# Late weight combinations in small steps, later stores, and output weights kept one chunk later, in a gated hybrid decoder step on one core

## The chip, the cores and the metric

The kernel runs on one core of a Trainium2 chip. The metric is the device time of one execution in microseconds (us). The engines are TensorE (PE, matmuls), VectorE (DVE), ScalarE (ACT), GpSimd (POOL) and SyncE (SP). All DMA transfers of this kernel are issued from SP's queue, which works in order: an issue that waits for its semaphore holds up everything behind it.

## The reference

One layer of a decoder step on 4096 prompt tokens (model width 1024) and 8 sample tokens, all in float32:

```python
h = rmsnorm(x) @ w_in        # columns: u | z_pool | q | k | v | z_attn | g_pool | g_attn
pooled  = multiscale_pool(u)                    # trailing means over 2/4/8/16, minus u itself
att     = sliding_window_attention(q, k, v)     # window 128, 8 query heads, 2 kv heads, sinks, T5 bias
br_pool = (grouped(pooled) * pool_scale * silu(z_pool)) @ w_br_pool
br_attn = (att * silu(z_attn)) @ w_br_attn
merged  = sigmoid(g_pool) * br_pool + sigmoid(g_attn) * br_attn
y       = rmsnorm(x + merged @ w_out)
```

The last keys, values and pool inputs are also outputs.

## The kernel before

**Precision.** A float32 product is made of three matmuls (lines 177 to 179, `mm3`): weights and activations are split into a rounded high part and a low part, and high x high, high x low and low x high are added up. `split_into` (lines 137 to 139) makes a weight's two parts: ACT casts the high part (line 138), DVE or POOL subtracts for the low part (line 139). A split weight tile `w` holds [128, 2, 4, 128], 512 KB; the raw tile `wr` that it comes from holds 256 KB.

**Chunks.** The prompt is worked through in eight chunks of 512 tokens; the second one also carries the eight sample tokens (520 columns, in two halves of 260). In each chunk the input projection is done in pairs of 128-column tiles. A pair is a 2 x 2 block product; `Pair` does it either with seven block products on combined weights (`s1` to `s4`, sums and differences of the raw blocks) and three plain blocks (`11`, `12`, `22`), or, for the pairs listed in `EIGHT` and in the first chunk only, with eight block products on plain weights. Each block product is 12 matmuls.

**Combined weights.** In the first chunk a seven-product pair loads its four raw blocks (line 193; tags `wr` and `wr0`, four buffers each, in turns), adds and subtracts them on DVE (line 198, scratch tag `sr`, one buffer), splits the results into `w` tiles, uses them, and `kept` stores them to DRAM (line 171, `ss<-w`). Later chunks load the stored 512 KB (line 167, `w<-ss`). For the four pairs in `EIGHT` the combined weights aren't used in the first chunk; `combine` makes them late in that chunk, one pair at a time, in split tiles with the tag `sc`, which has one buffer, and stores them (`ss<-sc`).

**Order within a chunk.** First K and V, Q, and the first A pair. Then eight fill stages (`FILL`): a projection pair on PE, into which attention scores, transposes and the value products of 128-token blocks are woven. In the first chunk these fill pairs make their combined weights on DVE and ACT, which also do the attention's element-wise work. Then come the gate pairs and the branch products `branch(0)` to `branch(7)` (line 854, `mm<-yph`, `mm<-yah`), and eight output tiles e = 0 to 7 (line 896, `mm<-mh`, with two weight tiles each). At each even e the next chunk's activations are prepared (`prep_xt`, lines 396 to 439).

**Output weights.** `kept` is used for them too: the first chunk splits each raw half and stores it (`so<-w`, 16 stores), and later chunks load 512 KB each (`w<-so`).

**Buffers.** Split weights share five `w` buffers; from the second chunk three more (`w2`) are used, in space that the first chunk's own pool (`wr0`, `sr`, `sc`) gives up when it is closed by `more_weights`.

A scheduler lays out each engine's instructions, in the order of the program where nothing else is ready sooner. Each engine then works through its list in order. A tile's buffer comes free when all that read it, stores included, are done.

The late calls stand in the branch loop and in the output loop of the first chunk:

```python
for j in range(KT):
    branch(j)
    if later and j > 4:
        combine(later.pop(0))
...
for e in range(KT):
...
    if later and e in (1, 3, 5):
        combine(later.pop(0))
```

Of the kernel before, what the change touches and what calls it, by code (L numbers as in the profile page):

```python
# [10 lines left out]
F32 = mybir.dt.float32  # L11
F32R = mybir.dt.float32r
AF = mybir.ActivationFunctionType
ALU = mybir.AluOpType
# [4 lines left out]
P = 128  # L19
# [16 lines left out]
W_U, W_Z, W_Q, W_K, W_V, W_A, W_GP, W_BR, W_GA, W_O = 0, 4, 8, 12, 13, 14, 18, 26, 34, 42  # L36
# [5 lines left out]
T_1, T_2, T_3, T_4, B_11, B_21, B_22 = range(7)  # L42
HB = TP // 2

EIGHT = [W_K, W_Q, W_U, W_U + 2]
SW = 16 + TP


def split_kernel(ctx, tc, i, o):
    nc = tc.nc  # L50
# [5 lines left out]
    dp = ctx.enter_context(tc.tile_pool(name="dp", bufs=1, space=DRAM))  # L56
# [6 lines left out]
    def st(shape, tag, bufs, dt=F32, nm=None):  # L63
        cnt[0] += 1
        return sp.tile(shape, dt, tag=tag, name=f"{nm or tag}_{cnt[0]}", bufs=bufs)
# [53 lines left out]
    def fst(shape, tag, bufs, dt=F32):  # L119
        cnt[0] += 1  # L120
        return p0.tile(shape, dt, tag=tag, name=f"{tag}_{cnt[0]}", bufs=bufs)
# [15 lines left out]
    def split_into(w, raw, eng=None):  # L137
        nc.scalar.copy(w[:, 0], raw)  # L138
        (eng or nc.vector).tensor_tensor(out=w[:, 1], in0=raw, in1=w[:, 0].bitcast(F32), op=ALU.subtract)  # L139

    def wtile():
        if "p1" in place:
            place["n"] += 1
            if place["n"] % 8 >= 5:
                cnt[0] += 1
                return place["p1"].tile([P, 2, 4, P], F32R, tag="w2", name=f"w_{cnt[0]}", bufs=3)
        return st([P, 2, 4, P], "w", 5, F32R)

    def wraw(idx, half):
        raw = st([P, 4, P], "wr", 4)  # L150
        nc.sync.dma_start(out=raw, in_=i["wall"][idx][:, 4 * half:4 * half + 4, :])
        return raw

    def wquarter(idx, half, eng=None):

        raw = wraw(idx, half)
        w = wtile()
        split_into(w, raw, eng)
        return w

    cache = {}

    def kept(key, make, own=False):

        w = fst([P, 2, 4, P], "sc", 1, F32R) if own else wtile()
        if key in cache:
            nc.sync.dma_start(out=w.bitcast(F32), in_=cache[key])
            return w
        split_into(w, make())
        cache[key] = dp.tile([P, 2, 4, P], F32, tag=f"s{key}", name=f"s{key}")  # L170
        nc.sync.dma_start(out=cache[key], in_=w.bitcast(F32))
        return w

    def mm3(ps, w, nk, rhs, start=True, stop=True, k0=0, **kw):
# [9 lines left out]
    def segs(c):  # L184
        return [(0, HB), (HB, TP)] if c == CS else [(0, T)]

    def combined(ia, ib, own=False):

        odd = own or len(cache) // 4 % 2
        raw = {}  # L190
        for idx, half in ((ib, 0), (ib, 1), (ia, 0), (ia, 1)):
            raw[idx, half] = fst([P, 4, P], "wr0", 4) if odd else st([P, 4, P], "wr", 4)
            nc.sync.dma_start(out=raw[idx, half], in_=i["wall"][idx][:, 4 * half:4 * half + 4, :])
        a11, a12, a21, a22 = raw[ia, 0], raw[ia, 1], raw[ib, 0], raw[ib, 1]
        s = fst([P, 4, P], "sr", 1)

        def add(o_, x, y, op):
            nc.vector.tensor_tensor(out=o_, in0=x, in1=y, op=op)
            return o_
        make = {"s1": lambda: add(s, a21, a22, ALU.add), "s2": lambda: add(s, s, a11, ALU.subtract),  # L200
                "s3": lambda: add(a21, a11, a21, ALU.subtract), "s4": lambda: add(s, a12, s, ALU.subtract)}
        plain = {"11": a11, "12": a12, "22": a22}
        return make, plain

    class Pair:
# [3 lines left out]
        def __init__(self, c, ia, ib, off=0, eng=None):  # L209
            self.c, self.ia, self.ib, self.eng = c, ia, ib, eng  # L210
            self.eight = c == 0 and ia in EIGHT
            self.pre = {}
# [104 lines left out]
    def first_tile(what, g):  # L317
        if what in ("gp", "ga"):
            return (W_GP if what == "gp" else W_GA) + 2 * g
        return {"a": W_A, "u": W_U, "z": W_Z}[what] + g  # L320

    def combine(ia):

        make, _ = combined(ia, ia + 1, True)
        for q in ("s1", "s2", "s3", "s4"):
            kept(f"{q}_{ia}", make[q], True)

    def pair(c, ia, **kw):
        p_ = Pair(c, ia, ia + 1, **kw)
# [44 lines left out]
    def prep_sq(c, parts, place_=None):  # L374

        if 0 in parts:
            state["ss"] = st([P, 10], "ss", 2)
        ss = state["ss"]
        for m in parts:
            t, half = m // 2, m % 2  # L380
            p = P if t < NB else NS
            xr = place_[m] if place_ else st([P, 4, P], "wr", 4).rearrange("p k c -> p (k c)")
            src = i["xq"][c, t] if t < NB else i["xn"]
            nc.sync.dma_start(out=xr[0:p], in_=src[:, half * T:(half + 1) * T])
            nc.scalar.activation(out=xr[0:p], in_=xr[0:p], func=AF.Square, accum_out=ss[0:p, m:m + 1])
# [244 lines left out]
    for c in range(NCH):  # L630
# [41 lines left out]
        w = TP if smp else T  # L672
# [12 lines left out]
        for j in (0, 2):  # L685
# [3 lines left out]
            if j == 0:  # L689
# [3 lines left out]
                for g in range(2):  # L693
# [4 lines left out]
                                                   in1=vs[:, 1:, g, r].bitcast(F32),  # L698
# [89 lines left out]
        def gate(which, p, **kw):  # L788
            idx = first_tile(which, p)
            return Pair(c, idx, idx + 1, **kw)  # L790

        later = list(EIGHT) if c == 0 else []

        def gate_done(which, p, h):
            nc.scalar.activation(out=h, in_=h, func=AF.Tanh, scale=0.5)
# [8 lines left out]
        for hb in range(2 * NB):  # L804
            what, g = FILL[hb]
            idx = first_tile(what, g)
            x = Pair(c, idx, idx + 1, off=16 if what == "u" else 0, eng=att)
# [25 lines left out]
        x = gate("ga", 1)  # L833
# [33 lines left out]
        gate_pair("gp", 2)  # L867
        for j in range(KT):
            branch(j)
            if later and j > 4:  # L870
                combine(later.pop(0))
            if nxt and j < 4:
                prep_sq(nxt, [2 * j, 2 * j + 1] + ([8, 9] if nxt == CS and j == 3 else []))
            if j == 1:
                gate_pair("ga", 2)
            if j == 3:
                gate_pair("gp", 3)
                gate_pair("ga", 3)
            if nxt and j == 4:
                prep_rs(nxt)  # L880
            if nxt and j == 5:
                state["rsb"] = rstd_bc(nxt, state["rs"])
# [3 lines left out]
        for e in range(KT):  # L886
            if e % 4 == 0:
                oy[e // 4] = big([P, 4, TP], F32, f"oy{e // 4}")
            if e % 2 == 0:
                xt = pair_tile()[:, :, 0:T]  # L890
                nc.sync.dma_start(out=xt, in_=i["xt"][c, :, e:e + 2, :])
            wo = [kept(f"o{e}_{half}", lambda: wraw(W_O + e, half)) for half in range(2)]
            for a, b in segs(c):
                ps = ps_mm(b - a)
                for half in range(2):
                    mm3(ps, wo[half], 4, lambda k: (mh[half][:, k, a:b], ml[half][:, k, a:b]),
                        start=half == 0, stop=half == 1)
                f = min(b, T)
                y = oy[e // 4]
                nc.vector.tensor_tensor(out=y[:, e % 4, a:f], in0=ps[:, 0:f - a], in1=xt[:, e % 2, a:f], op=ALU.add)  # L900
                if b > T:
                    nc.vector.tensor_tensor(out=y[:, e % 4, T:TP], in0=ps[:, f - a:], in1=xs0[:, e, :], op=ALU.add)
            n = w
            tail = c == NCH - 1 and e == KT - 1
            if e % 2 == 0 and c == NCH - 1 and e == KT - 2:
                sq = pair_tile()[:, :, 0:n]
                nc.scalar.activation(out=sq[:, 0], in_=y[:, e % 4, 0:n], func=AF.Square)
            if tail:
                nc.scalar.activation(out=sq[:, 1], in_=y[:, e % 4, 0:n], func=AF.Square)
            if e % 2 == 1:  # L910
                if not tail:
                    sq = pair_tile()[:, :, 0:n]
                    nc.scalar.activation(out=sq, in_=y[:, e % 4 - 1:e % 4 + 1, 0:n], func=AF.Square)
                if e == 1:
                    nc.vector.tensor_tensor(out=acc[:, 0:n], in0=sq[:, 0], in1=sq[:, 1], op=ALU.add)
                else:
                    for s_ in range(1 if tail else 2):
                        nc.vector.tensor_tensor(out=acc[:, 0:n], in0=acc[:, 0:n], in1=sq[:, s_], op=ALU.add)
                if c == NCH - 1 and e in (1, 5):
                    v = {1: 1, 5: 4}[e]  # L920
                    nc.scalar.activation(out=y[:, v % 4, 0:n], in_=y[:, v % 4, 0:n], func=AF.Identity,
                                         scale=gf[:, v:v + 1])
            if nxt and e % 2 == 0:
                prep_xt(nxt, e // 2)
            if later and e in (1, 3, 5):
                combine(later.pop(0))
        if c == 0:
            more_weights()
        final = (c, acc, oy, n)
# [72 lines left out]
```

## Time and profile before

| | us |
|---|---|
| median of 3 runs | 2447.07 |
| lowest, highest | 2443.22, 2449.73 |
| profiled execution | 2449.79 |
| its span | 2448.0 |

| engine | busy us (share of the span) |
|---|---|
| PE, matmuls | 2343.5 (96%) |
| PE, weight loads | 2180.9 (89%) |
| DVE | 1645.0 (67%) |
| ACT | 1152.9 (47%) |
| POOL | 312.2 (13%) |

The queue of dynamic transfers moved 587.09 MB, at a share of 70.2% of the 16 DMA engines. The mean granted TensorE clock was 0.987 of full speed. The first chunk ends at about 377 us of the span, where the first matmuls of the second chunk stand.

A line of an engine's timeline is read as: start us, duration us, engine, line of the kernel, operation, output <- inputs, shapes, count, and in brackets the idle time just before it with the instruction that ended it. A line of waits is: who waited <- for whom: total us, times, longest us. In a table of windows each row is a stretch of time with each engine's busy us and, in brackets, its instructions, and then the granted clock, the DMA share and GB/s.

### The profile page before, as it was taken

The numbers are of one execution on the slowest core, as the hardware profiler recorded it, in microseconds if no ns is written. First come the engines' busy times: TensorE is split into PE (matmuls) and PEld (weight loads), VectorE is DVE, ScalarE is ACT, GpSimd is POOL, SyncE is SP. The second block draws the span as 40 slices with busy tenths as digits, with TensorE's granted clock in tenths as the row PEclk, the third lists the DMA queues.
The fourth block names the chain that finished last, engine by engine and source line by source line (L and its number), as shares of the span: only waits on it lengthen the run. The fifth ranks groups of instructions, "written<-read, shape, count | busy, mean of one in ns | idle before, by whom it ended". The sixth has DMA issues, their size and how long they took to land.

```text
span 2448.0 us, 44073 instructions
## 1 busy us (share of the span) xinstructions
PE 2343.5 (96%) x16559; PEld 2180.9 (89%) x16559; DVE 1645.0 (67%) x3207; ACT 1152.9 (47%) x2346; POOL 312.2 (13%) x258
## 2 busy tenths in 40 slices
PE   7989968999999999999999999999999999999998
PEld 6988858999999988999889998899988998899996
DVE  7888866765567756686566765678557775568652
ACT  6666524564246632465334652356424564245531
POOL 1000000310014100230003300032000410013000
PEclk9999989999999999999999999999999999999998
DMA  6647898866687766866678666776677766677654
GB/s 225 216 172 250 282 311 310 233 241 234 213 272 257 245 221 228 299 234 225 224 245 288 234 236 224 241 278 231 239 236 244 273 224 236 238 281 242 219 191 146
DMA packets 235360, 589.90 MB, mean 241 GB/s; under 512 B 36699, under 2 KB 39036, under 8 KB 235148
## 3 DMA queue, kind: packets, MB, share of 16 engines
q1 hardware_dynamic: 235148, 587.09, 70.2%
q8 instruction: 131, 2.15, 0.4%
q14 instruction: 81, 0.66, 0.1%
HBM read 522.59 MB, written 64.40 MB: 240 GB/s over the span
## 4 chain that ended last, share of the span: by engine, by line
PE 69%; DVE 14%; DMA 9%; ACT 4%; issue 3%; SPq 0%; POOL 0%; DVEq 0%; ACTq 0%; POOLq 0%
PE hb L177 12%; PE hb L178 12%; PE hb L179 12%; PE mm L177 8%; PE mm L179 8%; PE mm L178 8%; DMA H<-in_xt 3%; DMA wr<-in_xq 3%; DVE w L139 2%; PE tp L485 2%; PE pv L496 2%; DMA wr<-in_wall 1%; DVE H L727 1%; DVE oy L618 1%; ACT w L138 1%
## 5 line engine op out<-in xcount | busy, mean ns | idle before, releaser
L177 PE MATMUL hb<-xt,w 128*128 128x256 f32 x3316 | 940.2, 284 | 33.4 <-DVE H L299 20.6
L179 PE MATMUL hb<-xt,w 128*128 128x256 f32 x3316 | 933.3, 282 | 4.8 <-DVE w L139 4.8
L178 PE MATMUL hb<-xt,w 128*128 128x256 f32 x3316 | 935.6, 282 | 0.3
L177 PEld LDWEIGHTS hb<-xt,w 128*128 128x128 f32 x3316 | 627.7, 189 | 44.5 <-DVE H L299 24.8
L179 PEld LDWEIGHTS hb<-xt,w 128*128 128x128 f32 x3316 | 629.3, 190 | 7.1 <-DVE w L139 6.5
L178 PEld LDWEIGHTS hb<-xt,w 128*128 128x128 f32 x3316 | 628.1, 189 | 3.7 <-DVE xt L182 1.5
L138 ACT CAST w<-wr 128x512 fp32r<-128x512 f32 x570 | 350.6, 618 | 340.6 <-PE hb L179 209.8
L139 DVE TENSOR_TENSOR w<-wr,w 128x512 fp32r<-128x512 f32 x402 | 275.3, 689 | 143.1 <-ACT w L138 138.8
L139 POOL TENSOR_TENSOR w<-wr,w 128x512 fp32r<-128x512 f32 x168 | 253.0, 1508 | 481.0 <-ACT w L138 384.7
L177 PE MATMUL mm<-mh,w 128*128 128x512 f32 (+1 forms) x576 | 216.5, 376 | 25.5 <-ACT w L138 24.6
L179 PE MATMUL mm<-mh,w 128*128 128x512 f32 (+1 forms) x576 | 215.5, 374 | 0.1
L178 PE MATMUL mm<-ml,w 128*128 128x512 f32 (+1 forms) x576 | 214.3, 372 | 0.0
L337 POOL TENSOR_TENSOR rs<-rs,nhalf 128x4 f32<-128x4 f32 (+1 forms) x18 | 18.0, 1002 | 1344.2 <-DVE rs L335 1344.2
L855 DVE SCALAR_TENSOR_TENSOR H<-H,mm 128x512 f32<-128x512 f32 (+1 forms) x144 | 90.3, 628 | 111.7 <-PE mm L179 111.2
L466 ACT ACTIVATE LL<-LL,nm 128x257 f32<-128x257 f32 (+1 forms) x256 | 126.5, 496 | 65.5 <-DVE nm L463 65.4
L177 PEld LDWEIGHTS mm<-mh,w 128*128 128x128 f32 x576 | 109.9, 191 | 46.3 <-ACT w L138 26.0
L423 ACT CAST xt<-H 128x256 fp32r<-128x256 f32 (+6 forms) x92 | 63.2, 687 | 169.3 <-DVE H L412 122.2
L177 PE MATMUL mm<-xt,w 128*128 128x260 f32 x476 | 135.5, 285 | 5.1 <-DMA w<-ss 3.0
L178 PE MATMUL mm<-xt,w 128*128 128x260 f32 x476 | 134.5, 283 | 0.0
L179 PE MATMUL mm<-xt,w 128*128 128x260 f32 x476 | 134.4, 283 | 0.2 <-DVE w L139 0.2
L900 DVE TENSOR_TENSOR oy<-mm,H 128x512 f32<-128x512 f32 (+1 forms) x72 | 45.2, 631 | 128.8 <-PE mm L179 91.1
L179 PEld LDWEIGHTS mm<-mh,w 128*128 128x128 f32 x576 | 109.5, 190 | 22.5 <-DVE w L139 1.7
(195 smaller groups left out, 4118.0 us busy)
## 6 DMA issues: line engine op xcount, KB each, us to landing
w<-ss SPq DMA_DIRECT2D x476, 512.0 KB
wr<-in_wall SPq DMA_DIRECT2D x585, 256.0 KB
w<-so SPq DMA_DIRECT2D x112, 512.0 KB
ss<-w SPq DMA_DIRECT2D x52, 512.0 KB
H<-in_xt SPq DMA_DIRECT2D x32, 512.0 KB
wr<-in_xq SPq DMA_DIRECT2D x56, 256.0 KB
H<-in_xt SPq DMA_DIRECT2D x56, 256.0 KB
out_y<-oy SPq DMA_DIRECT2D x28, 512.0 KB
```

Source lines behind the costliest of these rows:

```text
L138: nc.scalar.copy(w[:, 0], raw)
L139: (eng or nc.vector).tensor_tensor(out=w[:, 1], in0=raw, in1=w[:, 0].bitcast(F32), op=ALU.subtract)
L177: mm(ps, lhsT=w[:, 0, k0 + k, :], rhs=rh, start=start and k == 0, stop=False, **kw)
L178: mm(ps, lhsT=w[:, 0, k0 + k, :], rhs=rl, start=False, stop=False, **kw)
L179: mm(ps, lhsT=w[:, 1, k0 + k, :], rhs=rh, start=False, stop=stop and k == nk - 1, **kw)
L423: nc.scalar.copy(hi[:, s_], x)
L466: nc.scalar.activation(out=L[:, j, k0:2 * P + 1], in_=L[:, j, k0:2 * P + 1], func=AF.Exp, bias=nm[:, j:j + 1], accum_out=den[:, j:j + 1])
L485: nc.tensor.transpose(tp[:, j, :], L[:, j, kb * P:(kb + 1) * P], ident)
L496: mm(pv, lhsT=vs[:, b + kb, g, :], rhs=pt[:, kb, m].rearrange("p j q -> p (j q)"), start=n == 0 and m == 0, stop=n == len(kbs) - 1 and m == 1)
L618: nc.vector.scalar_tensor_tensor(out=y, in0=y, scalar=gf[:, e:e + 1], in1=rsp[:, 0:n], op0=ALU.mult, op1=ALU.mult)
L855: nc.vector.scalar_tensor_tensor(out=t[:, a:b], in0=t[:, a:b], scalar=1.0, in1=ps, op0=ALU.add, op1=ALU.mult)
L900: nc.vector.tensor_tensor(out=y[:, e % 4, a:f], in0=ps[:, 0:f - a], in1=xt[:, e % 2, a:f], op=ALU.add)
```

## The change

Four things are changed.

1. `EIGHT` loses its fourth pair (U+2, tiles 2 and 3 of the pool input). That pair is computed with seven products in the first chunk, like the others, and makes and stores its combined weights there.
2. For the three pairs that stay, `combine` becomes a generator that is advanced by `next`: twice after each of the branches 4 to 7, and once or twice after each output tile. One pair takes six steps: raw loads; two combinations; two more; the splits of `s1` and `s3`; their stores and the splits of `s2` and `s4`; the stores of these. The combinations are made in place in the raw tiles, the high parts go to tiles with the tag `sr` (now three buffers), and the low parts overwrite the raw tiles. High and low part are stored apart, 256 KB each. The tag `sc` is gone.
3. In `kept`, a new weight's store isn't issued at once but after the next new weight's split (`send`); the last one is sent at the chunk's end.
4. The first chunk's output weights are split and not stored; the second chunk splits them again and stores them; the third to eighth load them.

```diff
-EIGHT = [W_K, W_Q, W_U, W_U + 2]
+EIGHT = [W_K, W_Q, W_U]
...
+    unsent = []
+    def send():
+        for key, w in unsent:
+            nc.sync.dma_start(out=cache[key], in_=w.bitcast(F32))
+        unsent.clear()
-    def kept(key, make, own=False):
-        w = fst([P, 2, 4, P], "sc", 1, F32R) if own else wtile()
+    def kept(key, make):
+        w = wtile()
         if key in cache:
             nc.sync.dma_start(out=w.bitcast(F32), in_=cache[key])
             return w
         split_into(w, make())
+        send()
         cache[key] = dp.tile([P, 2, 4, P], F32, tag=f"s{key}", name=f"s{key}")
-        nc.sync.dma_start(out=cache[key], in_=w.bitcast(F32))
+        unsent.append((key, w))
         return w
...
-    def combined(ia, ib, own=False):
-        odd = own or len(cache) // 4 % 2
+    def combined(ia, ib):
+        odd = len(cache) // 4 % 2
...
-        s = fst([P, 4, P], "sr", 1)
+        s = fst([P, 4, P], "sr", 3)
...
-    def combine(ia):
-        make, _ = combined(ia, ia + 1, True)
-        for q in ("s1", "s2", "s3", "s4"):
-            kept(f"{q}_{ia}", make[q], True)
+    def combine(ias):
+        for ia in ias:
+            a = {}
+            for idx, half in ((ia + 1, 0), (ia + 1, 1), (ia, 0), (ia, 1)):
+                a[idx - ia, half] = fst([P, 4, P], "wr0", 4)
+                nc.sync.dma_start(out=a[idx - ia, half], in_=i["wall"][idx][:, 4 * half:4 * half + 4, :])
+            a11, a12, a21, a22 = a[0, 0], a[0, 1], a[1, 0], a[1, 1]
+            yield
+            tt = lambda o_, x, y, op: nc.vector.tensor_tensor(out=o_, in0=x, in1=y, op=op)
+            tt(a22, a21, a22, ALU.add)
+            tt(a21, a11, a21, ALU.subtract)
+            yield
+            tt(a11, a22, a11, ALU.subtract)
+            tt(a12, a12, a11, ALU.subtract)
+            yield
+            done = []
+            for q, s in (("s1", a22), ("s3", a21), ("s2", a11), ("s4", a12)):
+                hi = fst([P, 4, P], "sr", 3).bitcast(F32R)
+                nc.scalar.copy(hi, s)
+                nc.vector.tensor_tensor(out=s.bitcast(F32R), in0=s, in1=hi.bitcast(F32), op=ALU.subtract)
+                done.append((f"{q}_{ia}", hi, s))
+                if len(done) == 2:
+                    yield
+                    keep(done)
+            yield
+            keep(done)
+    def keep(done):
+        for key, hi, low in done:
+            cache[key] = dp.tile([P, 2, 4, P], F32, tag=f"s{key}", name=f"s{key}")
+            nc.sync.dma_start(out=cache[key][:, 0], in_=hi.bitcast(F32))
+            nc.sync.dma_start(out=cache[key][:, 1], in_=low)
+        done.clear()
...
-        later = list(EIGHT) if c == 0 else []
+        later = combine(EIGHT) if c == 0 else iter(())
...
             branch(j)
-            if later and j > 4:
-                combine(later.pop(0))
+            if j > 3:
+                next(later, None)
+                next(later, None)
...
-            wo = [kept(f"o{e}_{half}", lambda: wraw(W_O + e, half)) for half in range(2)]
+            wo = [kept(f"o{e}_{half}", lambda: wraw(W_O + e, half)) if c else wquarter(W_O + e, half)
+                  for half in range(2)]
...
-            if later and e in (1, 3, 5):
-                combine(later.pop(0))
+            next(later, None)
+            if e in (1, 2, 4):
+                next(later, None)
+        for _ in later:
+            pass
+        send()
```

## The prediction

> **What bounds the kernel now.** I read the page's forty slices first, then TensorE's (PE's) list of waits over the first 380 us, its timeline around the long waits, the chain through that stretch, and the windows.
>
> ```profile
> PE   7989968999999999999999999999999999999998
> ```
>
> Each digit is a 61 us slice. PE is at 9 nearly everywhere; the low digits all lie in the first seven slices, and the lowest behind the start are the sixth (306 to 367 us, 6) and the seventh (8). That is the end of the first chunk, where the change is.
>
> ```profile
> PE mm L177 <- ACT w L138: 24.8, 4, 13.2
> ...
> PE hb L179 <- DVE w L139: 4.8, 3, 2.6
> ...
> PE mm L177 <- DMA w<-ss: 1.7, 1, 1.7
> ```
>
> This list (total us, times, longest) says that 24.8 us go to matmuls that wait for a weight's ScalarE (ACT) cast. PE's timeline has them:
>
> ```profile
> 331.03 0.79 PE L177 MATMUL mm<-mh,w 128*128 128x512 f32 x1 [13.21 <-ACT w L138]
> ...
> 336.31 0.39 PE L177 MATMUL mm<-mh,w 128*128 128x512 f32 x1
> 336.54 0.40 PE L178 MATMUL mm<-ml,w 128*128 128x512 f32 x1
> ...
> 350.79 0.79 PE L177 MATMUL mm<-mh,w 128*128 128x512 f32 x1 [5.93 <-ACT w L138]
> ...
> 356.93 0.39 PE L179 MATMUL mm<-mh,w 128*128 128x512 f32 x1
> ...
> 370.51 0.79 PE L177 MATMUL mm<-mh,w 128*128 128x512 f32 x1 [5.51 <-ACT w L138]
> ...
> 373.98 0.40 PE L178 MATMUL mm<-ml,w 128*128 128x512 f32 x1
> ```
>
> Three gaps: 13.21 + 5.93 + 5.51 = 24.65 us. After each the matmuls start late too: warm they follow at 0.23 us (336.31 to 336.54), but from 331.03 to 336.31 there are 13 steps in 5.28 us, 14 steps in 6.14 us after the second gap, 7 in 3.47 us after the third. Against 0.233 us a step that is 2.25 + 2.88 + 1.84 = 7.0 us more. With the 1.7 us for a stored weight (w<-ss) at the next chunk's start the stretch holds 33.3 us.
>
> Why was the cast late? The chain:
>
> ```profile
> 307.24 4.53 DMA ss<-sc
> ...
> 314.99 6.11 DMA H<-in_xt
> ...
> 324.51 0.33 SPq L193
> ...
> 324.90 5.36 DMA wr<-in_wall
> ```
>
> and the stores of tile `sc`, with the waits for them:
>
> ```profile
> L171 SPq DMA_DIRECT2D ss<-sc x16: 319/326/335, 273.6 to 359.6; - x16
> ...
>   DMA ss<-sc: 14.3, 8
> ```
>
> The cast waited for a raw output weight whose load was issued only at 324.90, because SP's queue (in order) was standing at stores and reloads of the late combined pairs. Those go through one buffer `sc`: 16 stores from 273.6 to 359.6 us, one per 86.0 / 15 = 5.73 us (store 4.53, cast, subtraction), whatever PE does. PE's work in the stretch is shorter:
>
> ```profile
> 276.00:300.00 24.00, 24.00 (x108) 19.38 (x108) 20.98 (x35) 12.03 (x21) 0.32 (x2) 1.00 0.92 315
> 300.00:331.00 31.00, 17.82 (x77) 13.99 (x75) 21.79 (x36) 10.22 (x15) 0.97 (x4) 0.87 0.86 297
> 331.00:351.00 20.00, 14.04 (x49) 10.88 (x50) 14.11 (x24) 7.20 (x12) 0.36 (x1) 0.84 0.92 309
> 351.00:371.00 20.00, 14.49 (x49) 11.04 (x50) 10.73 (x19) 5.77 (x9) 0.77 (x2) 0.76 0.85 295
> ```
>
> (Columns: window, PE, weight loads, VectorE (DVE), ACT, POOL, clock, DMA share, GB/s.) PE is busy 70.35 of 95 us, about 63.4 of them at full clock. So the `sc` chain, not arithmetic, sets this stage.
>
> **The change, part by part.** *Late pairs.* `sc` goes; three pairs instead of four keep the high halves in three `sr` buffers and the low halves in the raw tiles, in steps dealt out from branch 4 to output tile 7. SP issues for them 12 raw loads and 24 stores of 256 KB; before it issued 16 and 16, and 16 output-weight stores: fewer, at 0.33 us each. The 16-link chain is gone: all 33.3 us are open to gain. What is late next? DVE in the four windows works 20.98 + 21.79 + 14.11 + 10.73 = 67.6 us. One pair less is 4 additions and 4 subtractions, which follow each other at 0.60 us:
>
> ```profile
> 232.30 0.68 DVE L863 SCALAR_TENSOR_TENSOR ml<-H,mh 128x512 fp32r<-128x512 f32 x1
> 232.90 0.69 DVE L139 TENSOR_TENSOR w<-wr,w 128x512 fp32r<-128x512 f32 x1
> ```
>
> so 4.8 us less: 62.8 us, beside PE's 63.4. And DMA:
>
> ```profile
> DMA packets 13762, 30.87 MB, mean 303 GB/s; under 512 B 3326, under 2 KB 3326, under 8 KB 13755
> ...
> so<-w SPq DMA_DIRECT2D x16, 512.0 KB
> ```
>
> From 270 to 372 us 30.87 MB moved. The 16 output-weight stores leave (8.4 MB), one pair's stores (2.1) and raw loads (1.05) too: 19.3 MB, at the 303 GB/s shown 64 us. Three resources of 63 to 64 us each cannot all be packed, and five in-order stops remain: ACT at the fourth high half of each of three pairs (its `sr` buffer is still being stored) and SP at the raw loads of the second and third pair (those buffers hold low halves on their way out). Bounds for what stays: 0, if look-ahead in five `w` buffers (12 x 0.233 = 2.8 us of PE each) covers all; 5 x 4.53 = 23 us, if every stop is a whole landing. I take 7, nearer the lower end, since DVE between 120 and 160 us (below) was packed to 99%. Late stage: -33.3 + 7 = -26.3 us.
>
> The clock is part of those 7:
>
> ```profile
> 190.92 0.38 PE L179 MATMUL hb<-xt,w 128*128 128x256 f32 x1 [1.17 <-DVE w L139]
> 191.14 0.28 PE L177 MATMUL hb<-xt,w 128*128 128x256 f32 x1
> ...
> 192.08 0.28 PE L179 MATMUL hb<-xt,w 128*128 128x256 f32 x1
> ...
> 194.03 0.58 PE L177 MATMUL hb<-xt,w 128*128 128x256 f32 x1 [1.67 <-ACT w L138]
> ...
> 195.14 0.41 PE L177 MATMUL hb<-xt,w 128*128 128x256 f32 x1
> ...
> 196.84 0.41 PE L179 MATMUL hb<-xt,w 128*128 128x256 f32 x1
> ```
>
> Two short gaps were enough here: steps go from 0.94 / 8 = 0.118 us to 1.70 / 8 = 0.213. I count 5.5 us of gaps and 1.5 of slow matmuls. The Trainium skill, "TensorE: Matmul & The Clock Gate", section "Why this matters for your kernels", asks only that no gap exceed about 3 us; the trace does not agree, as gaps of 1.17 and 1.67 us close together slowed PE. By that rule the gaps left would cost no clock, and the sum would be 1.5 us better.
>
> *Fourth pair (U+2) computed as seven products in the first chunk.* PE loses one product, 12 x 0.118 = 1.4 us. DVE gains four additions and three splits (7 x 0.60) and about 0.9 us of evacuation: 5.1 us. It lands in the fill of attention, where DVE is full:
>
> ```profile
> 120.00:140.00 20.00, 19.03 (x154) 18.17 (x152) 19.91 (x42) 13.90 (x32) 1.30 (x1) 1.00 0.42 145
> 140.00:160.00 20.00, 15.89 (x105) 13.11 (x106) 19.72 (x45) 11.75 (x27) 0.00 (x0) 1.00 0.40 145
> ```
>
> DVE 39.6 of 40 us, PE already 5 us short. Nothing hides DVE work there; the 1.4 us of PE don't count. +5 us (bounds -1.4, if earlier free DVE time takes it, and +7 with slow matmuls). The pair's four more 512 KB stores meet a DMA share of 0.4: nothing; without that slack each would be a landing late.
>
> *Stores one weight later.* SP no longer stands at a store whose subtraction has not run, so raw loads behind it go earlier; but 56 stored weights (14 pairs of four) hold their `w` buffer one or two weights longer. Today:
>
> ```profile
> ACT w L138 <- PE hb L179: 4.1, 7, 0.8
> ...
> ACT w L138 <- DMA ss<-w: 0.4, 1, 0.4
> ```
>
> In 60 to 245 us a store's landing ended one ACT wait, of 0.4 us. Beside attention a seven-product pair ends with line 310:
>
> ```profile
> 147.24 0.69 DVE L310 TENSOR_TENSOR H<-hb,U 128x512 f32<-128x512 f32 x1
> ...
> 199.85 0.69 DVE L310 TENSOR_TENSOR H<-hb,U 128x512 f32<-128x512 f32 x1 [1.78 <-PE hb L179]
> ```
>
> These are the first and the last of four, three pairs in 52.6 us: 17.5 us a pair, 2.5 a weight, so five buffers allow 12.5 us; split 1.3, a wait of 2.5 to 5.0 and a landing of 4.5 make 8.3 to 10.8: it fits. In the gate pairs without attention (84 x 0.118 = 9.9 us, 1.4 a weight, 7 us of life) it doesn't quite for the four stored of seven. Gain and loss bounded by -2 and +4 us; I take +1.
>
> *Output weights kept from the second chunk.* The first chunk loses 16 stores (counted). The second gains 16 casts (16 x 0.61 = 9.8 us ACT), 16 subtractions (9.6 DVE), 8.4 MB of stores, and reads 4.2 MB less:
>
> ```profile
> 612.00:640.00 28.00, 27.19 (x228) 26.98 (x226) 17.72 (x37) 6.95 (x11) 0.00 (x0) 1.00 0.59 202
> 640.00:680.00 40.00, 40.00 (x334) 40.00 (x335) 21.95 (x49) 8.96 (x12) 0.00 (x0) 1.00 0.70 236
> ```
>
> In 68 us DVE has 28 us free, ACT 52, and 4.2 MB add 62 GB/s to about 222. PE's own work hides it; without that cover it is up to 10 us. I take +1 for a start behind a late cast (0 to +4). The later chunks read stored weights as before.
>
> **Sum.** -26.3 + 5 + 1 + 1 = -19.3 us. The profiled execution took 2449.79 us (span 2448.0), 2.7 above the median of the runs, 2447.07; the same step from the median gives 2428.
>
> **Rivals.** *Landings take the chain's place.* The five stops are half exposed, and each exposed gap brings slow matmuls: 5 x 4.5 = 23 us left in place of 7, net -3: 2444. For it: the 14.3 us in which ACT stood at such stores before. Against it: 8.4 MB fewer, and steps an output tile apart (24 x 0.233 = 5.6 us of PE). By the fit of fixed and variable cost in the Trainium skill, "DMA: Bandwidth & Descriptors" (2.0 us and the bytes at 436 GB/s), I estimate 2.6 us for a 256 KB landing; then this rival leaves 13 us and gives 2434. The 5.36 us of a 256 KB load above don't agree.
>
> *Everything is covered.* No stop shows, and U+2's DVE work finds room: -33.3 - 1.4 + 2 = -32.7: 2414. For it: the second chunk's end, PE 67.2 of 68 us with the same matmuls; against it, DVE and DMA as full as PE.
>
> *Slower: the held buffers.* The delayed stores starve ACT of `w` buffers. Each of 56 weights then costs d; the gain is lost at d = 19.3 / 56 = 0.34 us, and the kernel is slower by over 0.3% (7.3 us) from 0.48. At 0.55 us it is +31, net +11.5: 2459. For it: in the gate pairs the buffer's life already exceeds the room by up to 3 us; against it: only the last four pairs run that fast, and PE would have to empty all five buffers each time.
>
> *The stretch stays full of transfers.* The raw loads are late because DMA is at a share of 0.9, whoever waits in the queue; PE then waits as before and the first chunk ends no sooner: 2442 to 2450, no change. Against it: 11.5 of 30.87 MB leave, and at 324.90 the load had not been issued.
>
> **How the numbers follow.** Forecast (-12 to -29 us) 0.60; covered 0.10; landings 0.18, spread from 2435 to 2448, a little over half of it faster by over 0.3%; unchanged 0.06; slower 0.06. I reckon 0.3% as what a measurement can tell. Faster: 0.60 + 0.10 + 0.10 and some of the unchanged case: 0.82; same 0.12; slower 0.06. The range goes from 2413 (covered) to 2443 (landings), with 2418 to 2435 the forecast's own.
>
> **What would show it.** In the changed trace: no `sc`; no PE wait over 4 us between 270 and 375 us, and three PE slices of 9 there; the first chunk ends some 20 us sooner; DVE near 100% from 115 to 160 us with some 5 us more PE waiting on DVE's w; the second chunk's end unchanged within 1 us, with 16 so<-w there. Wrong it would be by PE waits on ACT w behind stores of `sr` or raw tiles, or ACT w waits for ss<-w before 275 us.

## The result, and the profile after

The changed kernel takes 2418.2 us (median of 4 runs, 2414.14 to 2424.16), against 2446.86 us for the kernel before on the same chip: ratio 0.9889 [0.9871, 0.9907], or 28.7 us less. Its profiled execution took 2424.16 us (span 2422.4), 25.6 less than the profiled one before. All positions below are in profiled executions.

The forty slices of the changed kernel:

```profile
PE   7989999999999999999999999999999999999998
...
PEclk9989999999999999999999999999999999999999
```

The sixth and seventh digit of PE, 6 and 8 before, are 9. What stays low is the start, the third slice (121 to 182 us) and the end.

PE's waits of the changed kernel over the first 380 us (total us, times, longest):

```profile
PE tp L398 <- POOL rs L373: 13.0, 1, 13.0
PE hb L186 <- DVE w L139: 5.6, 5, 2.8
...
PE hb L184 <- ACT w L138: 3.6, 3, 1.7
...
PE mm L186 <- DVE w L139: 1.9, 3, 1.0
```

The longest of them is the kernel's start, which is not part of the change. The 24.8 us of output matmuls behind ACT's cast are gone; L184 to L186 are the three matmuls that had the lines 177 to 179. PE's timeline from the first output-tile matmul to the first matmul of the second chunk, with the gaps in it:

```profile
303.46 0.39 PE L184 MATMUL mm<-mh,w 128*128 128x512 f32 x1
...
309.46 0.50 PE L185 MATMUL mm<-ml,w 128*128 128x512 f32 x1 [0.64 <-DVE ml L899]
...
328.39 0.50 PE L186 MATMUL mm<-mh,w 128*128 128x512 f32 x1 [1.00 <-DVE w L139]
...
340.41 0.50 PE L186 MATMUL mm<-mh,w 128*128 128x512 f32 x1 [0.59 <-DVE w L139]
...
351.22 0.29 PE L184 MATMUL mm<-xt,w 128*128 128x260 f32 x1
```

The stretch of 192 output matmuls lasts 351.22 - 303.46 = 47.76 us, with 2.23 us of gaps; before it lasted 78.9 (298.13 to 376.99). At the 0.233 us a matmul of the undisturbed stretches 192 of them need 44.7 us. The same stretch as one window, before and then changed (PE, weight loads, DVE, ACT, POOL, clock, DMA share, GB/s):

```profile
298.00:377.00 79.00, 52.59 (x195) 40.03 (x193) 51.31 (x85) 26.43 (x39) 2.10 (x6) 0.83 0.86 294
```

```profile
303.00:351.00 48.00, 45.77 (x195) 36.01 (x194) 42.32 (x74) 19.92 (x31) 3.39 (x6) 1.00 0.79 267
```

PE works 45.77 of 48 us at full clock. The output weights are stored from the second chunk (tile `so` of the changed kernel):

```profile
L173 SPq DMA_DIRECT2D w<-so x96: 319/320/383, 885.1 to 2385.1; - x96
L166 SPq DMA_DIRECT2D so<-w x16: 319/326/422, 590.8 to 638.4; - x16
```

### The profile page after: what moved, and what is told of

Read it like the earlier page. It is cut to its first block, busy times and chain, and to the rows that moved or that the text cites. A ratio compares the mean times of both kernels' runs of the same rounds, so it can differ in the third digit from the quotient of the medians.

```text
span 2422.4 us, 44090 instructions
## 1 busy us (share of the span) xinstructions
PE 2336.5 (96%) x16547; PEld 2174.9 (90%) x16547; DVE 1650.7 (68%) x3224; ACT 1159.9 (48%) x2359; POOL 309.4 (13%) x258
## 4 chain that ended last, share of the span: by engine, by line
PE 69%; DVE 15%; DMA 8%; ACT 4%; issue 3%; SPq 0%; POOL 0%; DVEq 0%; ACTq 0%; POOLq 0%
PE hb L184 12%; PE hb L185 12%; PE hb L186 12%; PE mm L184 9%; PE mm L186 9%; PE mm L185 9%; DMA H<-in_xt 3%; DMA wr<-in_xq 2%; DVE w L139 2%; PE tp L521 2%; DMA wr<-in_wall 2%; PE pv L532 2%; DVE H L763 1%; DVE xt L189 1%; DVE oy L654 1%
## 5 line engine op out<-in xcount | busy, mean ns | idle before, releaser
L184 PE MATMUL hb<-xt,w 128*128 128x256 f32 x3312 | 938.7, 284 | 35.2 <-DVE H L306 22.7
L186 PE MATMUL hb<-xt,w 128*128 128x256 f32 x3312 | 931.1, 282 | 5.7 <-DVE w L139 5.6
L184 PEld LDWEIGHTS hb<-xt,w 128*128 128x128 f32 x3312 | 626.5, 189 | 47.0 <-DVE H L306 27.7
L186 PEld LDWEIGHTS hb<-xt,w 128*128 128x128 f32 x3312 | 627.7, 190 | 8.0 <-DVE w L139 8.0
L138 ACT CAST w<-wr 128x512 fp32r<-128x512 f32 x586 | 359.2, 617 | 338.4 <-PE hb L186 205.2
L139 DVE TENSOR_TENSOR w<-wr,w 128x512 fp32r<-128x512 f32 x418 | 285.7, 689 | 150.3 <-ACT w L138 147.1
L184 PE MATMUL mm<-mh,w 128*128 128x512 f32 (+1 forms) x576 | 213.3, 371 | 1.4 <-ACT mh L898 1.4
L186 PE MATMUL mm<-mh,w 128*128 128x512 f32 (+1 forms) x576 | 213.0, 370 | 1.6 <-DVE w L139 1.6
L891 DVE SCALAR_TENSOR_TENSOR H<-H,mm 128x512 f32<-128x512 f32 (+1 forms) x144 | 90.2, 627 | 108.4 <-PE mm L186 107.9
L184 PE MATMUL mm<-xt,w 128*128 128x260 f32 x476 | 135.6, 285 | 0.9 <-ACT U L300 0.5
L186 PE MATMUL mm<-xt,w 128*128 128x260 f32 x476 | 134.4, 283 | 0.6 <-DVE w L139 0.3
L186 PEld LDWEIGHTS mm<-mh,w 128*128 128x128 f32 x576 | 108.1, 188 | 22.8 <-DVE w L139 2.5
L185 PEld LDWEIGHTS mm<-ml,w 128*128 128x128 f32 x576 | 108.2, 188 | 21.7 <-DVE ml L899 1.9
L184 PEld LDWEIGHTS mm<-mh,w 128*128 128x128 f32 x576 | 108.1, 188 | 21.0 <-ACT mh L898 1.9
```

The lines of the kernel that those rows point to most:

```text
L184: mm(ps, lhsT=w[:, 0, k0 + k, :], rhs=rh, start=start and k == 0, stop=False, **kw)
L185: mm(ps, lhsT=w[:, 0, k0 + k, :], rhs=rl, start=False, stop=False, **kw)
L186: mm(ps, lhsT=w[:, 1, k0 + k, :], rhs=rh, start=False, stop=stop and k == nk - 1, **kw)
L891: nc.vector.scalar_tensor_tensor(out=t[:, a:b], in0=t[:, a:b], scalar=1.0, in1=ps, op0=ALU.add, op1=ALU.mult)
```

## The experiments

Four marks place each difference: **e0**, the first output-tile matmul of the first chunk; **c1**, the first matmul of the second chunk; **S**, the first attention score of the second chunk; and the end of the span. e0 to c1 is the stretch that the prediction called late. The column e0 to S adds the second chunk's opening, where what the late stretch left undone comes due.

| kernel | e0 | c1 | e0 to c1 | e0 to S | span | median | ratio to before |
|---|---|---|---|---|---|---|---|
| before | 298.1 | 377.0 | 78.9 | 130.2 | 2448.0 | 2447 to 2452 | 1 |
| changed | 303.5 | 351.2 | 47.8 | 99.4 | 2422.4 | 2418.2 | 0.9889 [0.9871, 0.9907] |
| changed, again | 304.0 | 352.2 | 48.2 | 102.6 | 2426.2 | 2423.2 | 0.9891 [0.987, 0.9912] |
| old, weights kept from 2nd | 304.1 | 354.1 | 50.0 | 109.3 | 2435.2 | 2433.14 | 0.9931 [0.9902, 0.996] |
| old with steps | 289.3 | 362.9 | 73.6 | 123.4 | 2432.9 | 2435.52 | 0.9938 [0.9918, 0.9958] |
| changed, weights kept from 1st | 302.9 | 368.9 | 66.0 | 115.4 | 2438.1 | 2441.68 | 0.997 [0.9955, 0.9986] |
| stores at once | 299.9 | 355.2 | 55.3 | 103.5 | 2422.5 | 2424.87 | 0.9902 [0.9872, 0.9932] |
| four late pairs | 295.1 | 354.4 | 59.3 | 109.0 | 2426.3 | 2428.19 | 0.9915 [0.9891, 0.9938] |
| four late pairs, dealt | 290.9 | 345.7 | 54.8 | 111.1 | 2423.4 | 2424.68 | 0.9896 [0.9877, 0.9916] |
| dummy stores, early | 304.2 | 350.5 | 46.4 | 99.2 | 2420.6 | 2423.7 | 0.9895 [0.9872, 0.9919] |
| dummy stores, late | 302.3 | 372.6 | 70.3 | 125.9 | 2448.0 | 2449.74 | 0.999 [0.9978, 1.0001] |
| stand without hold | 304.3 | 362.9 | 58.6 | 112.0 | 2432.7 | 2437.9 | 0.9944 [0.9926, 0.9963] |
| stores from POOL's queue | 302.2 | 362.5 | 60.3 | 112.2 | 2436.8 | 2439.52 | 0.9949 [0.9934, 0.9965] |
| POOL splits | 303.2 | 351.3 | 48.1 | 103.6 | 2425.0 | 2429.91 | 0.9912 [0.9896, 0.9928] |

The kernel before differed between chips (2446.86 to 2452.48), so kernels of different chips are compared by ratio. **Changed, again** is the same kernel once more:

> The changed kernel itself, on the chip of the next three, to compare them with. Both theories: 2414 to 2424.

The median of 2423.2 us is in that range. It shows how well a trace repeats: e0 and c1 within 1 us, S within 4. Differences below that are not read.

### One part undone or done alone

**The old kernel, output weights kept from the second chunk** (part 4 alone, the `sc` chain left in):

```diff
-wo = [kept(f"o{e}_{half}", lambda: wraw(W_O + e, half)) for half in range(2)]
+wo = [kept(f"o{e}_{half}", lambda: wraw(W_O + e, half)) if c else wquarter(W_O + e, half)
+      for half in range(2)]
```

> The kernel before with one thing changed: output weights kept from the second chunk (no stores of them in the first). Theory (chain): the three gaps stay for the most part, total 2440 to 2450, the 16 stores of sc still about 5 us apart. Rival (bytes): gaps mostly gone, total 2425 to 2432.

The theory failed: 2433.14 us lies below its range and just above the rival's, and the late stretch lasts 50.0 us. The chain, SP's waits (270 to 380 us), the raw output weights' loads and the stretch's window:

```profile
L171 SPq DMA_DIRECT2D ss<-sc x16: 319/326/344, 279.6 to 362.9; - x16
```

```profile
SPq L171 <- DVE sc L139: 34.5, 14, 4.7
```

```profile
310.10 0.33 SPq L151 DMA_DIRECT2D wr<-in_wall  x1
...
313.36 1.24 SPq L151 DMA_DIRECT2D wr<-in_wall  x2
...
319.68 0.42 SPq L151 DMA_DIRECT2D wr<-in_wall  x1
...
323.74 1.74 SPq L151 DMA_DIRECT2D wr<-in_wall  x3
```

```profile
304.00:354.00 50.00, 45.53 (x194) 35.68 (x192) 45.98 (x81) 22.26 (x34) 1.97 (x6) 1.00 0.82 274
```

The 16 stores of `sc` still follow each other every 83.3 / 15 = 5.55 us, and SP still stands 34.5 us for them. PE does not wait for it: the clock is 1.00, and the raw weights are loaded in time between the chain's links. So the chain by itself was not what held the output matmuls. It ends at 362.9, behind c1, and here the second chunk's opening (c1 to S) takes 59.3 us, against 51.6 and 54.4 in the two traces of the changed kernel. That the chain's end is the cause of this difference was not tested.

**The old kernel with the steps alone** (part 2; four late pairs, stores at once, output weights stored in the first chunk):

```diff
-EIGHT = [W_K, W_Q, W_U]
+EIGHT = [W_K, W_Q, W_U, W_U + 2]
...
+        send()                    # in kept, right behind unsent.append
...
-wo = [kept(...) if c else wquarter(W_O + e, half) for half in range(2)]
+wo = [kept(...) for half in range(2)]
```

(with one more step after each of the branches 4 to 7, so that four pairs are done in the same place)

> The kernel before with part 2 of the change alone: four late pairs in small steps with three sr buffers and no sc, dealt out as in the run above; stores at once, output weights stored in the first chunk. Theory (chain and transfers each hold the old stretch, and parts 2 and 4 are worth 10 and 13 to 16 us): 2436 to 2444. Rival 1 (with all 30.9 MB in the stretch the chain's end frees nothing): 2445 to 2452. Rival 2 (the chain was the cause of the gaps): 2420 to 2430.

2435.52 us is just below the theory's range and in neither rival's. The chain is gone, and the stretch is only 5.3 us shorter than before. SP's waits from 270 to 372 us, PE's from 270 to 385, and the window:

```profile
SPq L166 <- DVE w L139: 23.2, 13, 4.1
```

```profile
PE mm L185 <- ACT w L138: 16.6, 5, 6.2
```

```profile
289.00:363.00 74.00, 54.41 (x195) 40.13 (x195) 49.88 (x83) 25.46 (x39) 0.94 (x6) 0.88 0.93 321
```

Now SP stands 23.2 us at the stores of output weights (L166), and PE waits 16.6 us for casts (24.8 before). **The changed kernel with output weights stored in the first chunk** (part 4 undone) says the same from the other side:

```diff
-wo = [kept(...) if c else wquarter(W_O + e, half) for half in range(2)]
+wo = [kept(...) for half in range(2)]
```

> The changed kernel with the output weights stored in the first chunk again (16 stores of 512 KB back in the late stretch), the second chunk loading them. Theory (the one-buffer chain held the old stretch, bytes had little to do with it): late stretch 47.7 us plus 0 to 6, total 2418 to 2424. Rival (the stretch was full of transfers, and the 8.4 MB that left made the gain): plus 15 us or more, total 2433 or more, with PE waits on ACT w behind raw loads.

The rival came (2441.68 us), the theory did not. SP's waits (270 to 372 us), its timeline, and PE's row behind it:

```profile
SPq L166 <- DVE w L139: 21.9, 13, 4.7
```

```profile
299.75 1.83 SPq L151 DMA_DIRECT2D wr<-in_wall  x2
...
307.34 0.92 SPq L166 DMA_DIRECT2D so<-w  x2
...
318.73 0.65 SPq L151 DMA_DIRECT2D wr<-in_wall  x1
```

```profile
327.25 0.79 PE L184 MATMUL mm<-mh,w 128*128 128x512 f32 x1 [6.82 <-ACT w L138]
```

Between 299.75 and 318.73 no raw output weight is loaded; SP stands, then issues stores and the raw blocks of a late pair. It is the picture of the kernel before (loads at 304.64 and 324.90) without any `sc`. Undoing part 4 brings back 18.2 of the 31.1 us.

**Stores at once** (part 3 undone: `send()` right behind `unsent.append((key, w))`):

> The changed kernel with each stored weight sent right after its own split instead of one weight later. Theory (the delay is worth little either way): total 2415 to 2421, the first output tile within 2 us of 303.5. Rival 1 (an SP queue that stands at stores delays raw loads, and the delay cures it): 5 to 10 us slower. Rival 2 (held buffers cost time in the gate pairs): the first output tile 2 to 5 us sooner, total 2413 to 2416.

**Four late pairs** (`EIGHT` of four pairs again, part 1 undone; five of the 24 steps are left for the chunk's end), and the same **dealt** so that none is left (three steps after each branch, two after output tiles 0 to 4):

> The changed kernel with U+2 put back among the late pairs (four pairs in small steps, the last five steps at the chunk's end); everything else as changed. Theory (the move of U+2 cost about 5 us in the attention fill and buys room late): the first output tile starts near 298 us instead of 303.5, and the stretch from there to the second chunk grows from 47.7 us by 4 to 8 us, since DVE has 4.8 us more; total 2416 to 2422, no difference from the changed kernel. Rival (the late stretch has no room for a fourth pair): the stretch grows by 12 us or more with PE waits on ACT w above 8 us; total 2425 to 2432.

> As the four-late-pairs experiment, with the 24 steps dealt out so that the last falls on output tile 7 (three after each of branches 4 to 7, two after output tiles 0 to 4, then one). There the second chunk's first load stood 11.4 us behind the steps left over at the chunk's end. Theory (only those left-over steps made it slower; moving U+2 by itself is worth nothing): 2416 to 2422, the wait at the second chunk's start under 3 us. Rival (a fourth late pair costs transfers and DVE time wherever its steps are put): 2425 to 2432.

The intervals of all three (0.9902, 0.9915, 0.9896) overlap with those of the changed kernel (0.9889 and 0.9891), so no gain or loss of parts 1 and 3 is shown. The forecast ranges of theory and rival lie closer together than the kernel before differs between chips (5.6 us), so the medians in us (2424.87, 2428.19, 2424.68) don't decide either. What the marks show is work that changes its place. With stores at once e0 comes 3.6 us earlier, as its second rival has it, and the stretch is 7.5 us longer, 5.64 of them in one gap at 336.68 us; S stands where it stood. With four late pairs, dealt, e0 comes 12.6 us earlier and e0 to S takes 11.7 us longer. In the first of the two kernels with four late pairs the leftover steps stand ahead of the next chunk's weights in SP's queue:

```profile
354.36 0.58 PE L184 MATMUL mm<-xt,w 128*128 128x260 f32 x1 [11.44 <-DMA w<-ss]
```

### What of an output weight's store costs the time: bytes, standing or holding

A store moves 512 KB, makes SP stand until the split is done, and holds its `w` buffer until it has landed. The next four kernels start from the changed one.

**Dummy stores, early.** Two stores of constants (512 KB each) for each output tile of the first chunk:

```diff
+dummy = dp.tile([P, 2, 4, P], F32, ...)
+nc.sync.dma_start(out=dummy..., in_=bias[:, 0:4, :]...)
```

> The changed kernel plus 16 stores of 512 KB in the first chunk's output loop, two behind each output tile's weight loads, from a constant tile to scratch memory: the bytes and the queue entries of the old output-weight stores, without their wait for a subtraction and without holding a w buffer. Putting the real stores back cost 15.7 us of span. Theory B (bytes: the late stretch is limited by transfers): 10 to 18 us slower than the changed kernel, 2430 to 2440. Theory H (the stores hold w buffers until they land, and stand in SP's queue until DVE has subtracted): at most 4 us slower, 2414 to 2424.

This missed: constants depend on nothing, and the scheduler put the stores beside attention.

```profile
L934 SPq DMA_DIRECT2D d<-bias x16: 423/434/1187, 91.7 to 136.5; - x16
```

```profile
90.00:140.00 50.00, 43.19 (x315) 39.96 (x315) 42.70 (x96) 31.72 (x78) 1.59 (x3) 0.93 0.91 340
```

It says nothing on the late stretch, but something on the fill: there 8.4 MB more (share 0.91; 0.45 in the changed kernel) cost PE nothing, 43.19 us busy against 43.35.

**Dummy stores, late.** The same bytes, read from the output tile just finished, so that they can't go early:

```diff
+done_ = oy[(e - 1) // 4][:, (e - 1) % 4, 0:T] if e else ...
+for part in range(2): nc.sync.dma_start(out=dummy[:, part], in_=done_)   # for each half
```

> The changed kernel plus 8.4 MB of stores to scratch memory in the first chunk's output loop, each output tile's share read from the finished tile before it, so that they cannot be issued earlier (in the first try of this the queue's order put the 16 stores at 92 to 137 us, beside attention, where they cost nothing). The bytes of the old output-weight stores, without a w buffer held and without a wait for a subtraction. Theory B (transfers fill the stretch): 10 to 18 us slower than the changed kernel, 2432 to 2441. Theory H (holding and standing): within 4 us of it, 2419 to 2428.

```profile
303.00:373.00 70.00, 53.76 (x194) 40.95 (x193) 42.88 (x72) 20.79 (x31) 2.15 (x6) 0.83 0.89 311
```

```profile
SPq L936 <- DVE oy L944: 9.9, 6, 3.4
```

The whole gain is gone, with no weight held; but SP also stood 9.9 us at these stores, so bytes and standing are mixed. 2449.74 us lies above the ranges of both theories, and the ratio of 0.999 above the real stores' 0.997: these stores cost more than those whose bytes they copy, and why was not followed up.

**Stand without hold.** No output weight is stored, but SP waits for the same subtractions with a 32 KB store:

```diff
+mark = fst([P, 64], "mark", 2)
+nc.vector.tensor_copy(mark, wo[half][:, 1, 0, 0:64].bitcast(F32))
+nc.sync.dma_start(out=dummy, in_=mark)      # [P, 64], after each weight, first chunk
```

> The changed kernel plus, behind each output weight's subtraction in the first chunk, a copy of 64 columns of its low part into a small tile and a store of that tile (32 KB) from SP's queue: 16 queue entries that wait for the subtractions like the old stores, with hardly any bytes and no w buffer held. Theory S (SP standing at stores keeps the raw loads behind them late): 8 to 18 us slower than the changed kernel, 2431 to 2441, with waits of PE on ACT w above 8 us. Theory H (held buffers) and theory B (bytes): at most 4 us slower, of which 2 are the copies.

```profile
303.00:363.00 60.00, 51.94 (x200) 39.40 (x198) 46.92 (x92) 21.19 (x33) 7.67 (x6) 0.91 0.69 219
```

```profile
SPq L936 <- DVE mark L934: 17.1, 11, 6.0
```

Standing 17.1 us makes the stretch 10.8 us longer at 219 GB/s, less than the changed kernel moves (267). The 16 copies, which this kernel adds as well, keep DVE busy for 3.0 us in all, too little for the 10.8. Standing costs with hardly any bytes; 2437.9 us is in the range of Theory S, though PE's waits on ACT w are 6.1 us and not above 8.

**Stores from POOL's queue.** The output weights are stored in the first chunk, but POOL issues the stores:

```diff
-nc.sync.dma_start(out=cache[key], in_=w.bitcast(F32))
+(nc.gpsimd if key[0] == "o" else nc.sync).dma_start(out=cache[key], in_=w.bitcast(F32))
```

> The kernel with output weights stored in the first chunk (all else as changed), its 16 stores issued from POOL's queue instead of SP's: bytes and held buffers stay, SP no longer stands at them. From SP's queue it took 2441.7 us. Theory S (standing): back to 2420 to 2428. Theory H or B: 2435 to 2444.

```profile
303.00:363.00 60.00, 48.65 (x192) 37.53 (x191) 42.58 (x72) 21.64 (x32) 13.01 (x20) 0.91 0.93 338
```

```profile
ACT w L138 <- DMA wr<-in_wall: 8.1, 4, 6.0
```

SP does not stand at an output weight's store any more, and the stretch is still 12.5 us longer than the changed kernel's, 5.7 shorter than with the same stores on SP. DMA is at a share of 0.93, and the cast waits for a raw weight on its way (ACT, 290 to 370 us). So the bytes cost too, and 2439.52 us is in the range of Theory H or B. By their ratios: stores on SP 0.997, on POOL 0.9949, standing alone 0.9944, neither 0.9889 to 0.9891; against the latter some 20, 14 and 13 us of 2450, each known to some 4 us either way. Bytes and standing together seem to cost less than their sum. Holding was not taken away by itself, and the 14 us for bytes include it; the one wait that could be it, ACT for a store's landing in the kernel with POOL's stores, was 2.0 us.

### A version that might have been better

The lowest clock left is in the fill, where DVE splits. **POOL splits** gives POOL the subtraction of one plain block of each of these pairs:

```diff
-split_into(w, self.plain[q])
+split_into(w, self.plain[q], self.eng if q == "22" else None)      # eng = POOL in the first chunk's pairs
```

> The changed kernel with the low part of the last plain block (22) of each seven-product pair in the first chunk's attention fill subtracted on POOL instead of DVE: some 0.6 us less of DVE for each of seven pairs, where PE waits 15 us in all between 60 us and the first output tile. Theory (DVE bounds the fill, by row and instruction): 2 to 5 us faster than the changed kernel, 2418 to 2421. Rival (POOL's 1.5 us comes too late for the product, or slows DVE): no change or slower, 2423 to 2430.

0.9912 [0.9896, 0.9928]: no gain, as the rival has it. PE's waits for a subtraction from 85 to 290 us are

```profile
PE hb L186 <- DVE w L139: 7.5, 6, 2.9
```

against 5.6 in the changed kernel. None of the kernels tried beats the changed one.

## Why the prediction was right, and where not

**The sum.** Forecast: -19.3 us of span; measured -25.6 there and -28.7 in the medians; 2418.2 us lies in the range and at the lower edge of the forecast's own (2418 to 2435). By the marks: late stretch -26.3 forecast, -31.1 measured; up to e0 +6 (5 for U+2, 1 for the delayed stores), measured +5.3; second chunk onward +1, measured 0.2 (from S to the end 2019.6 us in both). That the total fits is in part luck: the stretch got short because the change also took away a second cause, which the prediction counted only as bytes and issues, and ahead of e0 two errors cancel. Both are worked out below.

**The term that was mis-sized** is the 7 us left over in the late stretch. What is left is 47.76 - 44.74 = 3.0 us: 2.23 of gaps and 0.8 of slower matmuls. The argument "Three resources of 63 to 64 us each cannot all be packed" and five in-order stops stood behind the 7 us. Over 48 us DVE is busy 42.32 and DMA at 0.79: the two were not full beside PE. The stops hardly show: from 270 to 372 us SP waits 1.9 us in all for raw tiles still being stored, and ACT 0.2 us for an `sr` buffer's store. Gaps of 1 us at most, over 10 us apart, left the clock at 1.00, so of the 1.5 us for slow matmuls 0.8 are left.

**The step that failed** is "So the `sc` chain, not arithmetic, sets this stage". The chain stood there in the trace, and SP did stand at it (14 times, 34.5 us, where the output matmuls did not suffer from it), but it was one of two occupants of the queue, and the prediction followed only one. With the chain kept and the output weights' stores taken away the stretch lasts 50.0 us; with the chain gone and those stores kept, 73.6 (before: 78.9, changed: 47.8). The prediction counted the 16 stores as 8.4 MB less to move and as 0.33 us each to issue; it did not ask for what SP waits at them, nor what is queued behind. The row for it was in the profile of before, from the same window in which I read `sc`. SP's waits before, 270 to 372 us:

```profile
SPq L171 <- DVE sc L139: 37.2, 15, 6.4
SPq L171 <- DVE w L139: 11.0, 8, 5.9
```

The second row is the output weights: 11.0 us of standing in eight stops, with raw weights behind. Size misled: the chain had three times as much.

**What each part brings** is read from e0 to S, in which the fill doesn't count; work that moves across e0 changes it too, so it is a reading and not a clean separation. Part 4: -20.9 us on the old kernel (130.2 to 109.3), -16.0 on the other three parts (115.4 to 99.4; -12.8 with the repeated trace). The steps in place of `sc`: -6.8 with the output weights' stores kept (130.2 to 123.4), nothing with them gone (109.3 to 111.1, four late pairs, dealt; the delayed stores are in that too). So part 4 makes the larger part of the stretch's gain, though the medians of the two alone look alike (0.9931 and 0.9938).

**They look alike because of what lies ahead of e0**, which moved without being meant to. e0 stands at 298.1 and 304.1 in the two kernels with the old late pairs, at 289.3, 290.9 and 295.1 in the three that have four pairs in steps. One thing of the change that serves the fill as well was costed nowhere: `sr` goes from one to three buffers, and `combined` makes its sums in it. DVE's waits for casts from 60 to 290 us, in the old kernel and in the old one with steps:

```profile
DVE w L139 <- ACT w L138: 13.2, 14, 2.8
```

```profile
DVE w L139 <- ACT w L138: 7.2, 9, 1.9
```

The other old fill with one buffer has 17.8 us there, the two other kernels with three buffers and four late pairs 9.0 and 7.3. The time from the first to the last attention score of the first chunk says the same: 107.5 and 107.9 us with one buffer, 103.6, 104.7 and 105.2 with three. That fits, but the buffers were not tried by themselves, so it stays open. It is also only a part: from the last of these scores to e0 the two old kernels take 109.8 and 112.7 us, the three 105.3 to 106.5, and no run says why.

U+2 as seven products shows in the same two figures. From the first to the last score the changed kernel takes 113.8 us (113.7 in the repeated trace), the kernel that differs in `EIGHT` alone 105.2, the dealt one 104.7. So the pair costs about 9 us in the fill, and not the 5 that I took, nor the 7 that I took as the bound. e0 moves by 8.4 and 12.6 us against these two. Since it moves by only 5.3 against the kernel before, the rest of the change gave 3 to 7 us back ahead of e0. The forecast of +6 there was right in its net only, which is luck. From e0 to S the two kernels take 9.6 and 11.7 us longer, so the fourth pair's move is worth nothing measurable in total.

**What would show it, point by point.** No `sc`, no PE wait over 4 us between 270 and 375, and three slices of 9: as said. The first chunk ends 25.8 us sooner, not 20. The second chunk takes 306.3 us (first matmul to first matmul of the third) before and after, with its 16 `so<-w`, and 305.5 in the changed kernel that stores them in the first chunk: part 4 costs nothing measurable there, as said. "DVE near 100% from 115 to 160 us" is wrong, and so are the 5 us more of PE waiting for DVE's w: over the first 380 us these waits are 5.6 us against 4.8. The windows of the changed kernel:

```profile
120.00:140.00 20.00, 15.76 (x104) 14.80 (x103) 16.10 (x35) 12.03 (x29) 0.54 (x1) 0.83 0.43 157
140.00:160.00 20.00, 14.06 (x91) 13.03 (x89) 17.29 (x36) 9.72 (x23) 0.00 (x0) 0.83 0.45 162
```

DVE went down from 39.6 to 33.4 of 40 us, and PE lost 5.1 us of work in them. DVE's longest waits there are for ACT (3.0 us for casts, 2.8 for the transposed probabilities): DVE was not full, and the engines waited for each other in turn. That POOL's help with the subtractions bought nothing fits with it.

**The rivals.** Landings in place of the chain did not come: PE has no wait over 1.00 us in the stretch. "Everything is covered" (2414) was nearer than the forecast in the late stretch, where 3.0 us were left and not 0, and wrong about a free place for U+2. Held buffers cost nothing that shows in the total: stores at once is not faster (0.9902), though its e0 comes 3.6 us sooner. "The stretch stays full of transfers" named a true cause, since the bytes cost some 14 us (holding included), and was wrong for this change because the change takes those bytes away.

## What to carry to other kernels

List everything that shares an in-order queue with a late transfer, and for each the wait at its head and what stands behind it; the longest line in the list of waits need not be the one that matters, since work with slack may wait for long at no cost. Move a store off a stage in which transfers fill the time to one with slack: at the second chunk's end the DMA share was 0.59 to 0.70 before the stores came there, it is 0.77 with them (586 to 640 us), and they cost nothing measurable. To judge the parts of a change, place marks along the span and compare between them, since a layout made anew shifts other stages by as much as the part is worth.

## What was not expected of the hardware

**Short gaps and the clock.** In the fill of the changed kernel:

```profile
128.53 0.38 PE L186 MATMUL hb<-xt,w 128*128 128x256 f32 x1 [2.05 <-DVE w L139]
...
131.64 0.58 PE L184 MATMUL hb<-xt,w 128*128 128x256 f32 x1 [1.67 <-ACT w L138]
...
147.91 0.51 PE L532 MATMUL pv<-PT,vs 128*128 128x512 f32 x1 [2.11 <-DVE PT L189]
...
151.26 0.58 PE L186 MATMUL hb<-xt,w 128*128 128x256 f32 x1 [2.85 <-DVE w L139]
```

No gap there reaches 3 us, and the two windows shown above (120 to 160 us) have a granted clock of 0.83. In finer windows it is 1.00 from 120 to 124 us, with 36 matmuls, and 0.50 from 132 to 136, just behind the first two gaps, with 20. The Trainium skill, "TensorE: Matmul & The Clock Gate", section "Why this matters for your kernels", asks for no idle gaps above about 3 us between bursts; here that is not enough, as gaps of 2.05 and 1.67 us that end 3.1 us apart cost clock as well.

**A second queue saves only its own standing.** POOL issues a store in 0.53 us where SP takes 0.32:

```profile
L166 POOL DMA_DIRECT2D so<-w x16: 533/533/772, 296.8 to 353.3; - x16
```

It gave back 5.7 us of the 18.2 in the stretch. The Trainium skill, "DMA: Bandwidth & Descriptors", section "Issuing engines are not separate DMA queues", says that transfers issued from several engines run on the same 16 DMA engines, so that only time on the issuing sequencer is saved. The trace agrees, with an addition in its numbers: the time saved on SP includes its standing at a semaphore, 21.9 us with the same stores on SP's queue.
